# Hybrid SSD block on one Trainium2 core: the last three projection pairs ordered product by product, two projection tiles moved from the direct form into a pair, and three steps of the scan drawn forward

## Chip, core and metric

The kernel runs on one core of one Trainium2 chip. The metric is the device time of one execution in microseconds. Before the change it is 1902.68 us (median of 3 runs, 1902.15 to 1902.8).

## The reference, cut to what matters

`x` has 1024 rows (time) and 1024 channels, all in float32:

```
u = rmsnorm(x) @ w_in                       # 1024 x 10272 columns, split into:
z, xbc, dt, s_b, s_c, s_x, g_a, g_b         # 2048, 3072, 32, then five of 1024
xbc = silu(causal_conv4(xbc) + b);  xs, B, C = split(xbc)
y = chunked_scan(xs, softplus(dt), a, B, C) + d * xs
y = group_rmsnorm(y * silu(z)) ;            branch_a = y @ w_ssd_proj
branch_b = (s_b * causal_conv3(s_c * s_x)) @ w_sconv_proj
h = x + (sigmoid(g_a) * branch_a + sigmoid(g_b) * branch_b) @ w_o
out = final_norm(h + (silu(n @ w_gate) * (n @ w_up)) @ w_down),  n = rmsnorm(h)
```

## The kernel before

**Precision and tiling.** Every large product is made of float32r matmuls on operands split into a high and a low half (`split`, or `hi` and `lo` of a pair: ScalarE, ACT in the profile, copies the high half, VectorE, DVE, subtracts to get the low one). One 128x128 by 128x512 block costs three matmuls: high by high, high by low, low by high (`mmc`, lines 680 to 682, and `mm3`, lines 81 to 83). The order of instructions on each engine is the order in which the Python program issues them; nothing is reordered later.

**Pairs.** Two neighbouring tiles of 128 columns of `w_in` form a `Pair`, which is computed with a seven-product scheme of the Strassen-Winograd kind instead of eight: products 1, 2, 6, 5, 7, 3, 4 of four k-blocks each, so 12 matmuls in one *slot*. The stationary side of a product is a sum of weight blocks (A1, S1 to S4, A2), made in `sums` on DVE and split in `hi` and `lo`; the moving side is one of the operands `T` (B11, B21, B22, T1 to T4) made once from the normalized rows. Products 1, 6, 7 and 4 accumulate into one PSUM bank (`b`), 2 and 5, 3 into another (`d`); `ev` takes the partial result out after each product (on ACT after 1, 6, 5, 4, on DVE after 2, 7, 3), and the next product on that bank waits for it. `slots` is the list of (pair, product); `STAGES` says how many slots ahead the sums, high and low halves are issued. The first three pairs run product by product (all product 1, then all product 2, ...), all others pair by pair. After product 3 and product 4 a finished tile goes to `side`, whose steps `pump` issues, one per slot: for a `z` pair that is one SiLU on ACT and a store (`silu_z`).

**The operands T.** They are made while the first pairs run, by the generator `second_half`, of which the dictionary `turns` takes steps after given slots (slot 9: B22, slot 11: T3, slot 14: T4). A second generator of that name does the same for the FFN.

**Direct tiles.** The last two `z` tiles and the sixteen gate tiles (`g_a`, `g_b`) are computed in the plain way, 2 halves x 8 k-blocks x 3 matmuls each, after all pairs. Beside them run the scan's steps: 32 items (4 groups x 8 chunks), each with `part1` (transposes, decay matrix by eight Relu and one Exp on ACT, five to six DVE operations) and, a step later, `part2` (state product `poff`, new state `pst`, diagonal `pdg`). `part1(j)` also issues item j+1's Relu and Exp. Steps are spread evenly over the direct matmul groups of three:

```
due = turn[0] * SCAN_STEPS // (len(direct) * 2 * KT - 4)
```

with SCAN_STEPS = 65 and 18 direct tiles (284). The scan's first step (loads) is issued once before them. After the direct tiles come the two output projections, `w_o`, and the FFN.

**Pages.** All large SBUF tiles come from one pool of 47 pages; a tile's page comes free after its last reader.

Of the kernel before, what the change touches and what calls it, by code (L numbers as in the profile page):

```python
# [10 lines left out]
AF = mybir.ActivationFunctionType  # L11
ALU = mybir.AluOpType

P = 128
S = 1024
D = 1024
KT = D // P
# [22 lines left out]
def hybrid_block(ctx: ExitStack, tc: tile.TileContext, x, nmw, w_in, cw, cb, dtb, alog, dsk, snw,  # L40
                 wssd, scw, wsc, wo, nfw, wg, wu, wd, fnw, out):
    nc = tc.nc
    ET = mybir.EngineType
    ctx.enter_context(tc.manual_schedule(engines={ET.PE, ET.Activation, ET.DVE, ET.Pool, ET.SP}))
    x, w_in, out = x[0], w_in[0], out[0]
# [14 lines left out]
    def page(s, shape=(P, 1024), dt=F32):  # L60
        return pp.tile(list(shape), dt, tag="pg", name=nm(s))
# [112 lines left out]
    def wslab(w, c0, cols=P, r0=0):  # L174
        return Slab(w[r0:r0 + D, c0:c0 + cols].rearrange("(k p) f -> p k f", p=P), (P, KT, cols))
# [45 lines left out]
    def every(gen):  # L221
        for _ in gen:
            pass
# [387 lines left out]
    def silu_z(i):  # L611
        def f(u):
            nc.scalar.activation(u, u, AF.Silu)
            nc.scalar.dma_start(z_d[i], u)
            yield
        return f
# [207 lines left out]
    def put(name, pages):  # L824
        T[name] = []
        for pg in pages:
            T[name].append(split(pg, "t", HB))
            yield
# [78 lines left out]
                side.append(self.done[1](self.u2))  # L907
                self.u2 = self.b = None

    z_pairs = [Pair(i * P, (silu_z(i), silu_z(i + 1))) for i in range(0, 14, 2)]  # L910
    x_pairs = [Pair(XBC0 + i * P, (conv_silu(i), conv_silu(i + 1))) for g in range(G)
               for i in (4 * g, 4 * g + 2)]
    bc_pairs = [Pair(XBC0 + i * P, (conv_silu(i), conv_silu(i + 1))) for i in (16, 18, 20, 22)]
# [7 lines left out]
    while conv_p or free_p:  # L921
# [2 lines left out]
        if free_p:  # L924
            rest_p.append(free_p.pop(0))
    pairs = first + rest_p
    NF = len(first)
    slots = [(p, n) for n in (1, 2, 5, 6, 7, 3, 4) for p in first] + \
        [(p, n) for p in rest_p for n in ORDER]


    STAGES = {1: ((2, "A1", 3), (0, "A1", 2)), 2: (), 6: ((1, "S3", 3), (1, "S2", 3), (2, "S2", 3), (0, "S2", 2)),
# [1 line left out]
              4: ((2, "A2", 4), (0, "A2", 3))}  # L934
    when = {}
    for i, (p, n) in enumerate(slots):
        for stage, what, d in STAGES[n]:
            if p not in first or what not in ("S3", "A1"):
                when.setdefault(i - d, []).append((stage, i, p, what))
        if p in first and n == 5:  # L940
            when.setdefault(i - 4, []).append((1, i, p, "S3"))
# [4 lines left out]

    loaded = [0]

    def load_pairs(n):
        while loaded[0] < min(n, len(pairs)):  # L950
            pairs[loaded[0]].y.load()
            pairs[loaded[0]].x.load()
            loaded[0] += 1
# [4 lines left out]
        p.ev(n)  # L958


    z_held = []

    def z_raw(i):
        def f(ps, hf):
            if hf == 0:
                z_held.append((i, page("gt")))
            nc.scalar.activation(z_held[-1][1][:, hf * 512:hf * 512 + 512], ps, AF.Copy)
            if hf and len(z_held) == 2:
                for k, t in z_held:
                    nc.scalar.activation(t, t, AF.Silu)  # L970
                    nc.scalar.dma_start(z_d[k], t)
                z_held.clear()
        return f

    direct = [(wslab(w_in, i * P), z_raw(i)) for i in range(14, 16)]
    for j in range(KT):
        direct += [(wslab(w_in, GA0 + j * P), gate_raw(ga_d[j])), (wslab(w_in, GB0 + j * P), gate_raw(gb_d[j]))]
    scan_steps = scans()
# [2 lines left out]
    def pump_scan(n=1):  # L981
        for _ in range(n):
            next(scan_steps, None)
# [6 lines left out]
    def direct_lo(slab):  # L990
        V.tensor_sub(slab.hl[1], slab.st, slab.hl[0].bitcast(F32))
        slab.st = None

    def direct_tile(i):
        slab, ev = direct[i]
        wh, wl = slab.hl
        slab.hl = None
        for hf in range(2):
            ps = bank("pr")
            for k in range(KT):  # L1000
                bh, bl = half_b(f"B{k // 4 + 1}{hf + 1}", k % 4)
                mm3(ps, wh[:, k, :], wl[:, k, :], bh, bl, k == 0, k == KT - 1)
                turn[0] += 1
                due = turn[0] * SCAN_STEPS // (len(direct) * 2 * KT - 4)
                if due > turn[1]:
                    turn[1] = due
                    pump_scan()
                if k % 8 == 5:
                    pump_aux()
                if i + 1 < len(direct) and (hf, k) == (0, 1):  # L1010
                    direct_hi(direct[i + 1][0])
                if i + 1 < len(direct) and (hf, k) == (0, 7):
                    direct_lo(direct[i + 1][0])
                if i + 2 < len(direct) and (hf, k) == (0, 2):
                    direct[i + 2][0].load()
            ev(ps, hf)
# [147 lines left out]
    def ffn_phase():  # L1164
# [27 lines left out]
        def second_half(rows):  # L1192
            yield from fill(rows, raw1, 1, wcol)
            t1 = [page("t1", HB) for _ in range(2)]
            for k in range(2):
                V.tensor_add(t1[k], raw1[0][k], raw0[0][k])
            t2 = [page("t2", HB) for _ in range(2)]
            for k in range(2):
                V.scalar_tensor_tensor(t2[k], raw1[1][k], -1.0, t1[k], op0=ALU.mult, op1=ALU.subtract)
            raw0[0].clear()  # L1200
            for k in range(2):
                nc.gpsimd.dma_start(raw1[0][k], raw1[1][k], accum_op=ALU.add)
            every(put("T2", t2))
            yield
            every(put("T1", t1))
            yield
            every(put("T3", raw1[0]))
            yield
            V.tensor_sub(raw0[1][0], raw0[1][0], t2[0])
            every(put("B22", raw1[1]))  # L1210
            yield
            V.tensor_sub(raw0[1][1], raw0[1][1], t2[1])
            every(put("T4", raw0[1]))
            yield

# [324 lines left out]
    rows_sq_on("v", a0, "x")  # L1540
    a1 = rows_acc(xt[4:8], "x")
    del xt
    for p in first:
        p.x.load(nc.gpsimd)
    pc = bank("pc")
    nc.tensor.transpose(pc[:, 0:96], ra, ident[:96, :96])
    nc.tensor.transpose(pc[:, 96:176], rb, ident[:80, :80])
# [41 lines left out]
    rows_sq_on("a", a1, "x")  # L1589
    p0.ev(1)  # L1590
    p2.hi("A1")
    p2.lo("A1")
    p2.pe(1)
    for k in range(4, 8):
# [11 lines left out]
    def second_half():  # L1606
        t1, t2 = [[page("t1", HB) for _ in range(2)] for _ in range(2)]
        for k in range(KT):
            if k % 2 == 0:
                raw1[k // 4].append(page("br", HB))  # L1610
            turn_rows(r1, k)
            pt = turned.pop(k)
            o = k % 4 // 2, k % 2
            nc.scalar.activation(raw1[k // 4][o[0]][:, o[1], :], pt, AF.Copy, scale=nmc[:, k:k + 1])
            less = (raw0[0] if k < 4 else t1)[o[0]][:, o[1], :]
            V.scalar_tensor_tensor((t1, t2)[k // 4][o[0]][:, o[1], :], pt, nmc[:, k:k + 1], less,
                                   op0=ALU.mult, op1=ALU.subtract)
            if k == 3:
                raw0[0].clear()
                for j in range(2):  # L1620
                    nc.sync.dma_start(b12_d[j], raw1[0][j])
                every(put("T1", t1))
            if k == 7:
                every(put("T2", t2))
            yield
        yield
        every(put("B22", raw1[1]))
        yield
        for k in range(2):
            V.tensor_sub(raw1[0][k], raw1[1][k], raw1[0][k])  # L1630
        every(put("T3", raw1[0]))
        raw1[0].clear()
        raw1[1].clear()
        yield
        for k in range(2):
            V.tensor_sub(raw0[1][k], raw0[1][k], t2[k])
        every(put("T4", raw0[1]))
        raw0[1].clear()
        yield
# [3 lines left out]
    for i in range(7 * NF):  # L1643
        if i >= NF:
            slot(i)
        make(i)
        for _ in range(turns.get(i, 0)):
            next(gen, None)
        if i == 2 * NF - 1:
            steps_pe(0, 1)  # L1650
        if i == 4 * NF - 1:
            steps_pe(1, 0)
            steps_pe(1, 1)
        load_pairs((i + 11) // 7 + 1)
        if i >= 4 * NF + 2:
            pump()
    every(gen)
# [7 lines left out]
        V.tensor_copy(cols[:, 176:192], pd2[:, 0:16])  # L1665

    sums = all_weight_sums()
    n_slots = len(slots)
    for i in range(7 * NF, n_slots):
        slot(i)  # L1670
        if i == 7 * NF + 4:
            time_steps(steps_ps)
            del steps_ps[:]
        if i == 7 * NF + 13:
            d_skip_rows()
        if i == 7 * NF + 14:
            d_skip_columns()
        make(i)
        load_pairs((i + 11) // 7 + 1)
        pump()  # L1680
        if i % 3 == 0:
            next(sums, None)
        if i % 3 == 1:
            pump_aux()
        left = n_slots - 1 - i
        if left in (4, 3, 2):
            del T[{4: "T2", 3: "T1", 2: "T3"}[left]]
        if left == 9:
            b12 = [page("br", HB) for _ in range(2)]
            for k in range(2):  # L1690
                nc.sync.dma_start(b12[k], b12_d[k])
        if left == 7:
            direct[0][0].load()
        if left == 4:
            every(put("B12", b12))
        if left == 3:
            direct_hi(direct[0][0])
            direct[1][0].load()
        if left == 2:
            direct_lo(direct[0][0])  # L1700
            pump_scan()
    every(sums)
    del T["T4"], b12
# [40 lines left out]
```

## Time and profile before

| | us |
|---|---|
| median of 3 runs | 1902.68 |
| the profiled execution | 1902.65 |
| its span, first to last instruction | 1900.8 |
| PE busy | 1875.0 |
| DVE busy | 1304.4 |
| ACT busy | 966.7 |
| direct tiles, first to last matmul | 636.8 to 949.7 |

PE is TensorE, PEld its weight loads, POOL is GpSimd, SP is SyncE (which issues most loads). The granted TensorE clock is 0.999 of full speed. A line number is that of the kernel before; L865 and L869 are the helpers `hi` and `lo` of a pair, L76 and L77 those of `split`.

### The profile page before, as it was taken

Reading aid. Unit: us, or ns where it says so; the run is one execution under the profiler, and the core shown is the slowest. Engines: PE = TensorE matmul, PEld = TensorE weight load, DVE = VectorE, ACT = ScalarE, POOL = GpSimd, SP = SyncE. Lnnn points to the kernel's source line nnn. Section 1 sums busy time; section 2 is a strip of 40 time slices with the busy share of each in tenths; the row PEclk is TensorE's granted clock in tenths of the full one; section 3 lists DMA queues with packets and bytes.
Section 4 is the critical chain, followed back from the end, with each engine's and each line's share of the span. In section 5 each row is a group of like instructions: output and inputs, shape, how many; then the busy total and the mean of one; then the engine's idle time right before and its main releaser. Section 6 shows DMA issues by size and latency. Waiting matters only on the chain. (4 is left out here: it accounts for less than half of the span.)

```text
span 1900.8 us, 24126 instructions
## 1 busy us (share of the span) xinstructions
PE 1875.0 (99%) x8893; PEld 1541.8 (81%) x8893; DVE 1304.4 (69%) x1694; ACT 966.7 (51%) x1541; POOL 177.3 (9%) x204
## 2 busy tenths in 40 slices
PE   6999999999999999999999999999999999999998
PEld 5788888888888888888888888888888888888886
DVE  7667888778685588999978558876444444456465
ACT  5545454444443788878665454464333333335333
POOL 2010111010100000010010000102211221100000
PEclk9999999999999999999999999999999999999999
DMA  5197999978958676688899665928988888867562
GB/s 182 58 265 173 242 230 236 233 190 230 267 143 233 225 247 213 225 273 263 281 323 333 221 211 203 232 82 199 212 198 210 202 192 196 235 258 283 188 196 109
DMA packets 336150, 413.02 MB, mean 217 GB/s; under 512 B 16408, under 2 KB 217840, under 8 KB 336032
## 3 DMA queue, kind: packets, MB, share of 16 engines
q1 hardware_dynamic: 277296, 302.43, 49.0%
q0 software_dynamic: 49664, 76.27, 21.6%
q10 hardware_dynamic: 9072, 32.77, 4.3%
q8 instruction: 70, 1.15, 0.2%
q14 instruction: 48, 0.39, 0.1%
HBM read 320.56 MB, written 143.15 MB: 244 GB/s over the span
## 5 line engine op out<-in xcount | busy, mean ns | idle before, releaser
L77 DVE TENSOR_TENSOR wl<-ws,wh 128x1024 fp32r<-128x1024 f32 x77 | 94.0, 1221 | 121.6 <-ACT wh L76 121.6
L680 PE MATMUL gb<-qh,gh 128*128 128x512 f32 x432 | 168.7, 391 | 0.1
L681 PE MATMUL gb<-ql,gh 128*128 128x512 f32 x432 | 168.4, 390 | 0.0
L682 PE MATMUL gb<-qh,gl 128*128 128x512 f32 x432 | 168.3, 389 | 0.0
L682 PE MATMUL fb<-th,wl 128*128 128x512 f32 x352 | 137.2, 390 | 0.5 <-DVE wl L77 0.5
L680 PE MATMUL fb<-th,wh 128*128 128x512 f32 x352 | 137.2, 390 | 0.0
L681 PE MATMUL fb<-tl,wh 128*128 128x512 f32 x352 | 137.1, 389 | 0.0
L681 PE MATMUL gd<-ql,gh 128*128 128x512 f32 x324 | 126.3, 390 | 0.0
L680 PE MATMUL gd<-qh,gh 128*128 128x512 f32 x324 | 126.2, 389 | 0.0
L682 PE MATMUL gd<-qh,gl 128*128 128x512 f32 x324 | 126.2, 389 | 0.0
L76 ACT ACTIVATE qh<-cb 128x1024 fp32r<-128x1024 f32 x98 | 99.9, 1019 | 38.8 <-PE gb L681 17.2
L81 PE MATMUL pr<-th,wh 128*128 128x512 f32 x288 | 118.8, 413 | 0.0
L77 DVE TENSOR_TENSOR ql<-cb,qh 128x1024 fp32r<-128x1024 f32 x98 | 115.7, 1181 | 2.8 <-ACT qh L76 2.7
L83 PE MATMUL pr<-th,wl 128*128 128x512 f32 x288 | 112.8, 392 | 0.0
L82 PE MATMUL pr<-tl,wh 128*128 128x512 f32 x288 | 112.6, 391 | 0.0
L680 PE MATMUL fd<-th,wh 128*128 128x512 f32 x264 | 102.8, 389 | 0.0
L682 PE MATMUL fd<-th,wl 128*128 128x512 f32 x264 | 102.8, 389 | 0.0
L681 PE MATMUL fd<-tl,wh 128*128 128x512 f32 x264 | 102.8, 389 | 0.0
L74 DVE SCALAR_TENSOR_TENSOR gl<-ca,gh 128x1024 fp32r<-128x1024 f32 (+1 forms) x60 | 70.6, 1176 | 44.1 <-ACT gh L73 44.0
L681 PE MATMUL pb<-tl,wh 128*128 128x512 f32 x248 | 96.9, 391 | 1.9 <-DVE tl L77 1.9
L680 PE MATMUL pb<-th,wh 128*128 128x512 f32 x248 | 97.7, 394 | 0.5 <-ACT u L895 0.5
L865 ACT ACTIVATE wh<-ws 128x1024 fp32r<-128x1024 f32 x62 | 65.7, 1059 | 63.5 <-DVE ws L852 59.6
(330 smaller groups left out, 4744.4 us busy)
## 6 DMA issues: line engine op xcount, KB each, us to landing
ws<-in_w_in_dram SPq DMA_DIRECT2D x75, 512.0 KB, 5.8
ws<-in_w_gate_dram SPq DMA_DIRECT2D x77, 256.0 KB, 3.9
ws<-in_w_up_dram SPq DMA_DIRECT2D x77, 256.0 KB, 4.4
ca<-u_d SPq DMA_DIRECT2D x35, 512.0 KB, 5.2
ab<-ac_d SPq DMA_DIRECT2D x32, 512.0 KB, 5.7
xbc_g<-cv ACTq DMA_DIRECT2D x24, 512.0 KB, 6.7
ws<-ws POOLq DMA_DIRECT2D x22, 512.0 KB, 6.4
wd_d<-in_w_down_dram SPq DMA_DIRECT2D x20, 512.0 KB, 10.3
```

Of the source, the lines that this page charges most:

```text
L74: nc.vector.scalar_tensor_tensor(lo, src, -1.0, hi.bitcast(F32), op0=ALU.mult, op1=ALU.subtract)
L76: nc.scalar.activation(hi, src, AF.Copy)
L77: nc.vector.tensor_sub(lo, src, hi.bitcast(F32))
L81: nc.tensor.matmul(o, lh, rh, start=first, stop=False)
L82: nc.tensor.matmul(o, lh, rl, start=False, stop=False)
L83: nc.tensor.matmul(o, ll, rh, start=False, stop=last)
L680: nc.tensor.matmul(o, lh, rh, start=first, stop=False, skip_group_check=True)
L681: nc.tensor.matmul(o, lh, rl, start=False, stop=False, skip_group_check=True)
L682: nc.tensor.matmul(o, ll, rh, start=False, stop=last, skip_group_check=True)
L865: nc.scalar.activation(t[0], self.source(what), AF.Copy)
```

## The change

It has six parts.

1. The last `z` tiles, 14 and 15, become an eighth `z` pair; the direct list holds the gates alone (16 tiles), and `z_raw` goes.
2. The last three pairs (all `z`) run product by product: 1, 2, 6 of the three, then 5 and 3 of different pairs in turn, then 7, then 4. `STAGES` of 3 and 7 are swapped for them (3 now comes first and needs S4), `load_pairs` loads them a pair every two slots, and T2, T1, T3 are freed at other slots.
3. Four steps of the scan instead of one are issued in these slots, when 10, 6, 3 and 0 slots are left; 62 steps are spread over 252 groups beside the direct tiles.
4. In the mixer's `second_half` the two subtractions that make T3 (L1630) move from the step of slot 11 to the end of the step of slot 9, behind B22's split.
5. In the FFN's `second_half` both subtractions for T4 (L1209 and L1212) are issued ahead of B22's split.
6. The second weight tiles (`x`) of the first three pairs are loaded from ACT's queue, after the high half of the third pair, instead of from POOL's queue before the constants are transposed.

```diff
-    z_pairs = [Pair(i * P, (silu_z(i), silu_z(i + 1))) for i in range(0, 14, 2)]
+    z_pairs = [Pair(i * P, (silu_z(i), silu_z(i + 1))) for i in range(0, 16, 2)]
...
-    NF = len(first)
+    NF, NL = len(first), 3
     slots = [(p, n) for n in (1, 2, 5, 6, 7, 3, 4) for p in first] + \
-        [(p, n) for p in rest_p for n in ORDER]
+        [(p, n) for p in rest_p[:-NL] for n in ORDER] + \
+        [(p, n) for n in (1, 2, 6) for p in rest_p[-NL:]] + \
+        [(rest_p[k - NL], n) for k, n in ((0, 5), (1, 5), (0, 3), (2, 5), (1, 3), (2, 3))] + \
+        [(p, n) for n in (7, 4) for p in rest_p[-NL:]]
...
-        for stage, what, d in STAGES[n]:
+        for stage, what, d in STAGES[{7: 3, 3: 7}.get(n, n) if p in rest_p[-NL:] else n]:
...
-    def load_pairs(n):
+    def load_pairs(i):
+        n, late = (i + 11) // 7 + 1, i + 11 - 7 * (len(pairs) - NL)
+        if late > 0:
+            n = len(pairs) - NL + 1 + late // 2
...
-    direct = [(wslab(w_in, i * P), z_raw(i)) for i in range(14, 16)]
+    direct = []
...
-                due = turn[0] * SCAN_STEPS // (len(direct) * 2 * KT - 4)
+                due = turn[0] * (SCAN_STEPS - 3) // (len(direct) * 2 * KT - 4)
...
-            V.tensor_sub(raw0[1][0], raw0[1][0], t2[0])
+            for k in range(2):
+                V.tensor_sub(raw0[1][k], raw0[1][k], t2[k])
             every(put("B22", raw1[1]))
             yield
-            V.tensor_sub(raw0[1][1], raw0[1][1], t2[1])
...
-    for p in first:
-        p.x.load(nc.gpsimd)
...
     p2.hi("A1")
+    for p in first:
+        p.x.load(nc.scalar)
...
         every(put("B22", raw1[1]))
-        yield
         for k in range(2):
             V.tensor_sub(raw1[0][k], raw1[1][k], raw1[0][k])
+        yield
         every(put("T3", raw1[0]))
...
+    T_LAST = {12: "T2", 8: "T1", 3: "T3"}
+    EARLY = (10, 6, 3, 0)
...
-        if left in (4, 3, 2):
-            del T[{4: "T2", 3: "T1", 2: "T3"}[left]]
+        if left in T_LAST:
+            del T[T_LAST[left]]
...
         if left == 2:
             direct_lo(direct[0][0])
+        if left in EARLY:
             pump_scan()
```

## Rows read from the trace of the kernel before

**Rows 1.** The page, busy time of each engine, share of the span, instructions.

```profile
PE 1875.0 (99%) x8893; PEld 1541.8 (81%) x8893; DVE 1304.4 (69%) x1694; ACT 966.7 (51%) x1541; POOL 177.3 (9%) x204
```

**Rows 2.** PE's waits: who released it, us in total, times, longest.

```profile
PE pb L681 <- DVE tl L77: 1.9, 2, 1.1
...
PE poff L476 <- ACT st L483: 0.6, 1, 0.6
...
PE fb L682 <- DVE wl L77: 0.5, 1, 0.5
```

**Rows 3.** Timeline of PE where the direct tiles begin: start, duration.

```profile
636.84 0.39 PE L81 MATMUL pr<-th,wh 128*128 128x512 f32 x1
...
637.52 0.39 PE L81 MATMUL pr<-th,wh 128*128 128x512 f32 x1
```

**Rows 4.** Timeline of all engines, 12.4 to 13.6 us.

```profile
12.09 0.91 POOL L165 DMA_DIRECT2D ws<-in_w_in_dram  x1
...
12.30 0.95 DVE L137 TENSOR_SCALAR xn<-x,nr 128x512 f32<-128x512 f32 x1
...
13.17 0.95 DVE L137 TENSOR_SCALAR xn<-x,nr 128x512 f32<-128x512 f32 x1
```

**Rows 5.** Timeline of DVE, 15.9 and 34 to 36 us.

```profile
15.80 0.47 DVE L137 TENSOR_SCALAR xn<-x,nr 128x512 f32<-128x512 f32 x1
...
34.26 1.21 DVE L845 TENSOR_TENSOR ws<-ws,ws 128x1024 f32<-128x1024 f32 x1
```

**Rows 6.** Timeline of PE, its transposes of the first rows.

```profile
14.27 4.93 PE L1557 MATMUL pt<-ident,xn 128*128 128x128 f32 x30 [0.49 <-DVE xn L137]
```

**Rows 7.** Timeline of ACT, 8 to 10 us; ACTq is its issuing side.

```profile
8.36 1.30 ACTq L245 DMA_DIRECT2D x<-in_x_dram  x3
```

**Rows 8.** Timeline of DVE, 64 to 79 us (slots 9 to 12).

```profile
66.82 1.22 DVE L869 TENSOR_TENSOR wl<-ws,wh 128x1024 fp32r<-128x1024 f32 x1
...
69.83 1.23 DVE L869 TENSOR_TENSOR wl<-ws,wh 128x1024 fp32r<-128x1024 f32 x1 [1.19 <-ACT wh L865]
...
71.57 2.35 DVE L1630 TENSOR_TENSOR br<-br,br 128x1024 f32<-128x1024 f32 x2
```

**Rows 9.** Timelines of ACT and of PE, 72 to 76 us.

```profile
72.89 2.19 ACT L76 ACTIVATE th<-br 128x1024 fp32r<-128x1024 f32 x2
...
75.26 0.50 PE L681 MATMUL pb<-tl,wh 128*128 128x512 f32 x1 [0.76 <-DVE tl L77]
```

**Rows 10.** Timeline of DVE in the FFN's start.

```profile
1303.66 1.22 DVE L1212 TENSOR_TENSOR br<-br,t 128x1024 f32<-128x1024 f32 x1
```

**Rows 11.** Timeline of ACT, the scan's first steps.

```profile
640.10 2.43 ACT L399 ACTIVATE ab<-ab,pac 128x128 f32<-128x128 f32 x8
642.55 1.28 ACT L401 ACT_TABLE_LOAD   x1
643.85 1.06 ACT L401 ACTIVATE ab<-ab 128x1024 f32<-128x1024 f32 x1
...
649.38 1.06 ACT L401 ACTIVATE ab<-ab 128x1024 f32<-128x1024 f32 x1
...
656.36 0.58 ACT L483 ACTIVATE st<-pst 128x512 f32<-128x512 f32 x1
```

**Rows 12.** Timeline of DVE, the same steps.

```profile
645.10 0.29 DVE L444 TENSOR_TENSOR cbm<-pcb,caus 128x128 f32<-128x128 f32 x1 [2.93 <-ACT bh L437]
...
647.25 1.22 DVE L991 TENSOR_TENSOR wl<-ws,wh 128x1024 fp32r<-128x1024 f32 x1
```

**Rows 13.** Windows: busy time and instructions of PE, PEld, DVE, ACT, POOL.

```profile
800.00:950.00 150.00, 150.00 (x954) 123.60 (x953) 141.63 (x242) 116.08 (x275) 14.38 (x23) 1.00 0.82 275
```

**Rows 14.** Timelines of ACT and PE, the state of items 24 to 26.

```profile
885.51 0.58 ACT L483 ACTIVATE st<-pst 128x512 f32<-128x512 f32 x1
...
886.58 0.60 PE L476 MATMUL poff<-bc,st 128*128 128x128 f32 x4
...
896.45 0.72 PE L476 MATMUL poff<-bc,st 128*128 128x128 f32 x5
```

More of the change, by code (lines that the diff above doesn't have):

```diff
@@ L958, in slot @@
         p.ev(n)
[L961 to L973, printed above, removed]
-    direct = [(wslab(w_in, i * P), z_raw(i)) for i in range(14, 16)]
+    direct = []
     for j in range(KT):
@@ L1653, in hybrid_block @@
             steps_pe(1, 1)
-        load_pairs((i + 11) // 7 + 1)
+        load_pairs(i)
         if i >= 4 * NF + 2:
@@ L1678, in hybrid_block @@
         make(i)
-        load_pairs((i + 11) // 7 + 1)
+        load_pairs(i)
         pump()
```

## The prediction, made before the changed kernel was run

> **What bounds the kernel.** The page comes first: PE is busy for 1875.0 of 1900.8 us, DVE for 1304, ACT for 967 [rows 1]. So time goes only where PE gets less to do or waits less. PE's list of waits is the second view: all that it waits for after the first 20 us are single waits of a microsecond or less, and three of them touch this change: for the low half of T3 (one of the two under L681), for the scan's state, and for a weight's low half in the FFN [rows 2]. The third view is PE's timeline, and it corrects a trap: a matmul is drawn 0.39 us long, but the next but two starts 0.68 us later [rows 3], so one costs 0.227 us, and a slot of 12 costs 2.72. The remaining views are the timelines of DVE and ACT around the places that the change touches, since both work in program order and PE waits for whatever stands late in them. The sum is made against the profiled execution's 1902.65 us (its span of 1900.8 and 1.85 around it), 0.03 from the median.
>
> **Part 1, the eighth pair.** Two direct tiles are 2 x 2 x 8 x 3 = 96 matmuls, a pair is 7 x 12 = 84. Twelve fewer at 0.227 us: -2.7 us. By the drawn 0.39 us it would be -4.7; the starts decide. ACT also loses four copies and DVE one low half net, neither of which PE waits for.
>
> **Part 6, the early loads.** The rows show a half of the normalization (L137) that takes 0.95 us and ends just when a load issued by POOL does, twice in a row [rows 4]; the last one, after POOL's last issue, takes 0.47 [rows 5]. With the three `x` loads gone from POOL, the one at 12.30 still waits (for the third pair's `y`), the one at 13.17 no longer. PE's long run of transposes, released at 14.27 by that half [rows 6], starts some 0.57 us earlier (it needs the half's end, 13.64 rather than 14.12 or so, and what lay between); PE's wait for the first low half follows it. I take -0.6; the bounds are 0 and -1.5 (three halves at 0.48 saved). The Trainium skill says the same of the cause: in "SBUF — State Buffer", section "SBUF: two separate sides", VectorE in its two-port mode and GpSimd exclude each other for whole instructions. By that rule too a half is freed entirely or not at all, which these durations bear out. On ACT the three issues take 1.30 us on its issuing side, which runs beside the computing one [rows 7]; if it did not, ACT's next copy would come 1.3 us later, the upper bound for this part. The `x` tiles are first needed by the subtraction at 34.26 [rows 5], some 9 us after their new issue near 24; I price that at nothing. If DVE did have to wait there, PE's transposes behind it would be late next.
>
> **Part 4, T3's subtractions.** They go ahead of three things in DVE's queue: the low half at 66.82, the sum that lets ACT make the next pair's high half, and the low half at 69.83, for which DVE waited 1.19 us on ACT [rows 8]. In before the two subtractions (71.57, 2.28 from start to start) ran while ACT made the last of the high halves, and T3's own high half followed at 72.89 [rows 9]. Now the sum, the high half, the low half and the next sum all slide by 2.28, the high half of the third pair with them, and T3's split stands behind that on ACT. So T3's low half is ready 2.28 us later, not sooner, and the wait that ended at 75.26 (about 1.0 us) becomes 3.3: +2.2 us. The bounds are -1.0 (the wait goes altogether, if ACT or DVE has room that I do not see) and +2.3.
>
> **Part 5, the FFN's subtractions.** The second one, at 1303.66 [rows 10], goes in front of B22's split, where DVE idled for most of its length; T4's split and the weight's low half behind it come 0.9 us sooner, and the wait of 0.5 under L682 [rows 2] (0.6 with its restart) goes: -0.6, bounds 0 and -0.6.
>
> **Parts 2 and 3, the scan's steps among the last slots.** The order by product gives every bank at least as much time as before; the list of waits shows nothing there to win. The cost is the scan's: its second step occupies ACT from 640.10 to the end of the Exp at 649.38, 10.2 us, and the third step 5.5 us more [rows 11]; DVE sits at L444 until 5.0 us into the first [rows 12], and 2.15 us of work follow. Set the clock to zero where PE ends the last product 3 (6 slots left). DVE's add and the SiLU behind it take until 2.0, the ACT block until 12.2. PE has the three products 7 (8.2) and twice 0.76 of transposes, so product 4 of the first pair runs from 9.7 to 12.4. For the second pair ACT's high half of A2 stands behind the block (12.8) and DVE's low half follows (13.5): 0.6 of waiting. For the third, the take-out of product 7 stands on DVE behind the low halves of B12, whose high halves end on ACT at 15.2: it is done at 17.3, PE wants it at 15.8. With crumbs +2.2 us. Bounds: 0, if ACT runs ahead by a few slots more than I set, and +5, if the third step's 5.5 us get into the same path. Next, the state's copy (L483), for which PE waits already, 0.6 idle and 0.2 of restart [rows 2, 11]: now it stands behind the third step, three take-outs, three SiLUs and a table load, some 1.5 us behind PE, so +0.7; bounds -0.8 and +2.
>
> Of table loads the row shows 1.28 us, with the Exp at once behind [rows 11]; SiLU and Exp alternate twice in these slots. The Trainium skill, "ScalarE: Activation LUTs", sections "What ACT_TABLE_LOAD costs" and "Table sets: the hidden batching unit", speaks against such alternating and prices a switch at 2.66 us, of which 1.38 are a drain. By that page the sum would be 2.8 us higher; the row has no such drain, so the sum stays.
>
> **The denser scan.** 62 steps over 252 groups are one in 4.06 instead of 4.37; an item is two steps, so its period falls by 0.62 groups of 0.68, from 9.87 us (poff to poff [rows 14]) to some 9.45, 4.3% less. From 800 to 950 us DVE is busy for 141.6 of 150 [rows 13]; the same work gets about 143.6. It fits barely; the state's copy ends 0.49 us before PE takes it at 886.58 [rows 14], and in such places 0.4 less period and a growing lag show. I take +1.3 us. Bounds 0 and +5.9 (0.42 an item over 14 items, if none of DVE's gaps closes).
>
> **The sum.** -2.7 - 0.6 + 2.2 - 0.6 + 2.2 + 0.7 + 1.3 = +2.5, rounded up for steps left out: 1905.3 us.
>
> **Rivals.** *Everything is hidden*: DVE and ACT run ahead of PE by more than I set, so neither burst reaches it and the T3 wait and the state's wait vanish: -2.7 - 0.6 - 1.0 - 0.6 - 0.8 = -5.7, 1897.0 us. For it: all waits in before are short. Against it: the chain through ACT and DVE at 66 to 73 us is serial [rows 8, 9]. *DVE becomes the bound beside the direct tiles*: it decides from the point where its lag passes the 0.49 us at item 25, and the price is 5.9 instead of 1.3: 1909.9, slower. For it: 94% busy there already [rows 13]. Against it: gaps that partly close. *A table switch costs its drain too*: ACT's block and the copies behind it lengthen by 1.4 each time, 1908.1 us; no row speaks for it. The page named above is its source. *Page waits*: a new page whose last reader is late holds DVE or a load in the last slots, 1908 or so; no row shows one.
>
> **Chances and range.** The forecast 0.45, all hidden 0.20, DVE the bound 0.28, table drain 0.02, page waits 0.05. A measurement of this kernel can tell 0.2%, 3.8 us: faster is below 1898.9, slower above 1906.5. The forecast lies between, so faster 0.20, same 0.45, slower 0.35. The range takes in both outer cases to about their middle, 1897.0 to 1909.5; the forecast's own is 1902.5 to 1907.
>
> **What would show it.** 8881 matmuls for 8893. PE's long transposes start near 13.7. The low half of T3 releases PE near 77.0 instead of 75.26, after a wait near 3 us. No wait under L682 in the FFN. Waits of 0.5 to 1.5 us at product 4 of the second and third of the last pairs, released by DVE, and one near 1.5 at the first poff. Waits at poff of items 25 and 31, and DVE above 97% in the last third of the direct tiles. I am wrong if the T3 wait shrinks, if PE runs through the last slots without a wait, or if DVE makes PE wait at many poffs.

## The result, and the profile after

The changed kernel takes 1911.67 us (median of 6 runs, 1909.81 to 1916.19) against 1902.64 of before beside it: a ratio of 1.0048, 95% interval 1.0038 to 1.0058. It is slower, by 9.0 us, and 2.2 above the upper end of the range; the forecast was 1905.3. The profiled execution took 1916.19 us, 13.5 more than that of before, and is the slowest of the six, so its rows hold more than the median does.

First the page and PE's list of waits after (us in total, times, longest; not all lines), which answer to [rows 1, 2]:

```profile
PE 1879.6 (98%) x8881; PEld 1541.4 (81%) x8881; DVE 1309.8 (68%) x1704; ACT 969.4 (51%) x1544; POOL 174.7 (9%) x201
```

```profile
PE poff L476 <- ACT st L483: 3.6, 2, 2.7
...
PE pb L681 <- DVE tl L77: 1.9, 2, 1.1
PE pb L680 <- ACT th L76: 1.8, 1, 1.8
PE pb L680 <- DVE u L900: 1.7, 2, 1.3
```

PE executes 12 matmuls fewer and yet is busy 4.6 us longer: matmuls themselves got slower somewhere. PE's timeline shows where, behind the wait for T3:

```profile
75.25 0.49 PE L680 MATMUL pb<-th,wh 128*128 128x512 f32 x1 [1.81 <-ACT th L76]
76.51 0.50 PE L681 MATMUL pb<-tl,wh 128*128 128x512 f32 x1 [0.77 <-DVE tl L77]
...
77.78 0.63 PE L680 MATMUL pb<-th,wh 128*128 128x512 f32 x1
78.21 0.63 PE L681 MATMUL pb<-tl,wh 128*128 128x512 f32 x1
...
80.77 0.58 PE L681 MATMUL pb<-tl,wh 128*128 128x512 f32 x1
81.19 0.40 PE L682 MATMUL pb<-th,wl 128*128 128x512 f32 x1
```

From 77.78 to 81.19 eight matmuls start 0.427 us apart, where 15 would fit at 0.227: a loss of 8 x 0.2 = 1.6 us. The windows (busy time and instructions of PE, PEld, DVE, ACT, POOL, then the granted clock, DMA share, GB/s) give the clock, half of full speed, 1.2 GHz, in this stretch and in two more:

```profile
77.70:81.10 3.40, 3.40 (x10) 2.67 (x9) 0.52 (x1) 0.55 (x1) 0.00 (x0) 0.51 0.00 0
675.10:678.50 3.40, 2.97 (x11) 2.54 (x11) 1.88 (x4) 3.38 (x9) 0.00 (x0) 0.50 0.97 324
955.00:958.40 3.40, 3.40 (x20) 2.74 (x17) 3.26 (x7) 0.00 (x0) 0.00 (x0) 0.50 0.51 196
676.00:954.00 278.00, 273.53 (x1749) 224.29 (x1749) 254.22 (x435) 227.63 (x546) 18.21 (x28) 1.00 0.76 248
```

Each of the three is 3.41 us long. The first and the third begin within 1.3 us behind a wait of PE, the second in the last 0.45 us of one. The second and third cost 1.4 and 1.6 us against the same instructions at full clock in `after_again`, a second profiled execution of the change (below). By the Trainium skill, "TensorE: Matmul & The Clock Gate", section "HAM oscillation — how this bites in real kernels", the loss is half of the throttled time, by which one would estimate 1.7 us for each. The rows come close to it. Before had no such stretch until its last microseconds.

The waits at product 4 of the last three pairs, and the first matmul behind the third one:

```profile
653.37 0.47 PE L680 MATMUL pb<-th,wk 128*128 128x512 f32 x1 [0.48 <-DVE u L900]
...
660.87 0.47 PE L680 MATMUL pb<-th,wk 128*128 128x512 f32 x1 [1.26 <-DVE u L900]
...
663.77 0.39 PE L81 MATMUL pst<-xw,bh 128*128 128x512 f32 x1
```

They stand at the first and the third pair. From 653.37 the 36 matmuls take 10.40 us, where 8.2 would do at 0.227; with the 0.7 us of the first wait and its restart product 4 loses 2.9 us.

The waits at the scan, on PE's timeline (the poff of items 1, 25, 27 and 31, and the start of a tile):

```profile
675.53 0.79 PE L476 MATMUL poff<-bc,st 128*128 128x128 f32 x2 [2.72 <-ACT st L483]
...
897.54 1.16 PE L476 MATMUL poff<-bc,st 128*128 128x128 f32 x8 [0.91 <-ACT st L483]
916.97 1.16 PE L476 MATMUL poff<-bc,st 128*128 128x128 f32 x8 [1.00 <-ACT gt L657]
925.33 0.50 PE L81 MATMUL pr<-th,wh 128*128 128x512 f32 x1 [0.85 <-ACT gt L657]
...
953.71 1.16 PE L476 MATMUL poff<-bc,st 128*128 128x128 f32 x8 [1.70 <-DVE st L485]
```

What lay ahead of the first of them on ACT (start, duration; ACTq is its issuing side), which answers to [rows 11]:

```profile
667.35 0.58 ACT L906 ACTIVATE u<-pb 128x512 f32<-128x512 f32 x1
667.94 1.28 ACT L613 ACT_TABLE_LOAD   x1
669.24 1.06 ACT L613 ACTIVATE u<-u 128x1024 f32<-128x1024 f32 x1
...
673.42 1.06 ACT L613 ACTIVATE u<-u 128x1024 f32<-128x1024 f32 x1
...
674.88 0.60 ACT L483 ACTIVATE st<-pst 128x512 f32<-128x512 f32 x1 [0.40 <-ACT u L613]
```

Three take-outs, a table load and three SiLUs stand between the Exp and the 0.6 us copy that PE waits for. The waits at 917 and 925 come from one more place, ACT's wait of 5.2 us for a page that a store of POOL still held (in before ACT never waits for that store):

```profile
910.94 0.63 ACT L441 ACTIVATE xw<-xx 128x512 fp32r<-128x512 f32 x1 [5.23 <-DMA yt_d<-y]
```

And this is DVE in front of the last wait:

```profile
949.50 1.22 DVE L74 SCALAR_TENSOR_TENSOR gl<-ca,gh 128x1024 fp32r<-128x1024 f32 x1
950.64 1.22 DVE L77 TENSOR_TENSOR ql<-cb,qh 128x1024 fp32r<-128x1024 f32 x1
951.78 0.68 DVE L471 TENSOR_TENSOR st<-st,cd 128x512 f32<-128x512 f32 x1
952.38 0.68 DVE L477 TENSOR_TENSOR xx<-poff,eb 128x512 f32<-128x512 f32 x1
952.98 0.68 DVE L485 TENSOR_TENSOR st<-st,pst 128x512 f32<-128x512 f32 x1
```

L74 and L77 are the low halves of the first chunk *behind* the direct tiles; its first matmul, at 963.93, reads them 12 us later. They stand ahead of the state (L471, L485) that PE takes at 953.71.

### The profile page after: what moved, and what is told of

Same layout as the page of the kernel before. It is cut to its first block, busy times and chain, and to the rows that moved or that the text cites. A ratio compares the mean times of both kernels' runs of the same rounds, so it can differ in the third digit from the quotient of the medians.

```text
span 1914.3 us, 24111 instructions
## 1 busy us (share of the span) xinstructions
PE 1879.6 (98%) x8881; PEld 1541.4 (81%) x8881; DVE 1309.8 (68%) x1704; ACT 969.4 (51%) x1544; POOL 174.7 (9%) x201
## 5 line engine op out<-in xcount | busy, mean ns | idle before, releaser
L77 DVE TENSOR_TENSOR wl<-ws,wh 128x1024 fp32r<-128x1024 f32 x77 | 94.0, 1221 | 121.6 <-ACT wh L76 121.6
L77 DVE TENSOR_TENSOR ql<-cb,qh 128x1024 fp32r<-128x1024 f32 x98 | 115.6, 1179 | 1.7 <-ACT qh L76 1.6
L81 PE MATMUL pr<-th,wh 128*128 128x512 f32 x256 | 106.6, 416 | 0.9 <-ACT gt L657 0.9
L680 PE MATMUL pb<-th,wh 128*128 128x512 f32 x256 | 101.6, 397 | 2.3 <-ACT th L76 1.8
L680 PE MATMUL pb<-th,wk 128*128 128x512 f32 x256 | 100.0, 391 | 2.0 <-DVE u L900 1.7
L74 DVE SCALAR_TENSOR_TENSOR gl<-ca,gh 128x1024 fp32r<-128x1024 f32 (+1 forms) x60 | 70.5, 1174 | 44.2 <-ACT gh L73 44.1
L83 PE MATMUL pr<-th,wl 128*128 128x512 f32 x256 | 100.4, 392 | 0.0
```

Of the source, the lines that this page charges most:

```text
L74: nc.vector.scalar_tensor_tensor(lo, src, -1.0, hi.bitcast(F32), op0=ALU.mult, op1=ALU.subtract)
L77: nc.vector.tensor_sub(lo, src, hi.bitcast(F32))
L81: nc.tensor.matmul(o, lh, rh, start=first, stop=False)
L83: nc.tensor.matmul(o, ll, rh, start=False, stop=last)
L680: nc.tensor.matmul(o, lh, rh, start=first, stop=False, skip_group_check=True)
```

## The experiments

Ratios are to before, with 95% intervals; the median of before was 1902.8 to 1903.1 in each set.

**The parts alone.** `t3_alone` is before with part 4, `no_t3` the change without it:

```diff
         every(put("B22", raw1[1]))
-        yield
         for k in range(2):
             V.tensor_sub(raw1[0][k], raw1[1][k], raw1[0][k])
+        yield
         every(put("T3", raw1[0]))
```

> The kernel before with part 4 alone (T3's two subtractions moved into slot 9's step). First theory, serial queue: the wait for T3 grows from 1.1 to about 3.1 us, +2.0 us, and if the granted clock falls to its lower level behind that wait, as it does at 77.7 us in the changed kernel, another 1.6: 1904.6 to 1906.3 us, with the granted clock of the run telling which. Rival, the subtractions are out of the way sooner: the wait goes, 1901.6 us. Second rival, the wait was there from something else that the whole change did: 1902.6 us, unchanged.

> The changed kernel with part 4 alone undone. First theory, waits add up and a long one costs clock too: 2.0 us less, or 3.6 less where the clock fell: 1908.0 to 1909.7 us, no half-clock stretch near 78 us. Rival, all that matters is the dense scan beside the direct tiles: 1911.7 us, unchanged.

t3_alone took 1906.42 (1.0017, 1.0008 to 1.0026), no_t3 1909.65 (1.0034, 1.0022 to 1.0047). T3's waits in the first:

```profile
75.55 0.50 PE L680 MATMUL pb<-th,wh 128*128 128x512 f32 x1 [1.83 <-ACT th L76]
76.81 0.50 PE L681 MATMUL pb<-tl,wh 128*128 128x512 f32 x1 [0.76 <-DVE tl L77]
77.14 0.39 PE L682 MATMUL pb<-th,wl 128*128 128x512 f32 x1
77.37 0.39 PE L680 MATMUL pb<-th,wh 128*128 128x512 f32 x1
```

The waits are those of the change, and here no half clock follows: starts stay 0.23 apart. Of the 11 runs three (the profiled one among them) lie at 1904.4 to 1905.1 with a mean clock of 0.999, eight at 1906.1 to 1907.3 with 0.998: the means of the groups (1904.7 and 1906.7) are 2.0 us apart, near the price of one fall.

`no_early` issues one scan step early, as before, and 65 beside the 16 tiles; `parts56` is before with parts 5 and 6 alone:

```diff
-    EARLY = (10, 6, 3, 0)
+    EARLY = (2,)
...
-                due = turn[0] * (SCAN_STEPS - 3) // (len(direct) * 2 * KT - 4)
+                due = turn[0] * SCAN_STEPS // (len(direct) * 2 * KT - 4)
```

> The changed kernel with a single early scan step (two slots before the end, as before the change), so 65 steps over 252 groups. First theory, the scan's burst among the last slots costs 2.4 us there and 2.9 at the first poff (with the clock 1.6 more): these waits go, but the direct tiles lose more than the 5.1 us of now, some 7; together 1907 to 1909 us. Rival, DVE alone is the bound beside the direct tiles, and the early steps only relieve it: three steps of about 8 us of DVE work come back into the stage, and the time rises to 1914 us or more.

> The kernel before with parts 5 and 6 alone (FFN subtractions and the x loads on ACT's queue). First theory: 0.8 us less at the start and 0.6 less in the FFN, 1901.2 us. Rival, the gain at the start is lost again at the next waits of DVE and ACT: 1902.0 us; second rival, nothing: 1902.6 us.

parts56 took 1901.33 (0.9991, 0.9983 to 1.0000), as expected. no_early took 1918.99 (1.0083), 10 us above its theory and in the range of its rival, DVE as the bound. In it the waits at product 4 are gone and the first poff's is 0.3, so the early steps do cause them; at the poffs of items 25 and 31 PE waits far longer:

```profile
PE poff L476 <- DVE st L485: 5.3, 1, 5.3
PE poff L476 <- ACT st L483: 3.7, 2, 3.3
```

**First theory beside the tiles: DVE's rate.** `two_rates` spreads the 62 steps unevenly, `light_dve` leaves out the second of the two additions into y, `state_dve` moves one copy to DVE:

```diff
-                due = turn[0] * (SCAN_STEPS - 3) // (len(direct) * 2 * KT - 4)
+                t0 = turn[0]
+                due = t0 * 32 // 122 if t0 <= 122 else 32 + (t0 - 122) * 30 // 130
```

```diff
-        for i in range(2):
+        for i in range(1):
             o = slice(i * 2 * P, i * 2 * P + 2 * P)
```

```diff
-                nc.scalar.activation(ns, pst, AF.Copy)
+                (V.tensor_copy if j == 0 else lambda o, i: nc.scalar.activation(o, i, AF.Copy))(ns, pst)
```

> The changed kernel, with its 62 scan steps spread unevenly over the same 252 groups of the direct tiles: 32 in the first 122 (one in 3.8) and 30 in the last 130 (one in 4.3, about as before). The work of each engine is the same. Theory (the waits at the poffs of items 25 and 31 and at 917 and 925 us come from the period in the stretch behind item 16, where the norms come on top and DVE is above 97% busy): these four waits, 5.1 us with their restarts, shrink to under 1.5 in all, and the fall of the clock behind the last goes; 1906 to 1908.5 us against 1911.7. Rival (they come from the total of DVE's work beside the tiles, so a faster first half only moves the lag forward): waits of 3 us or more in all remain or appear before item 16, 1910 us or more.

> The changed kernel, leaving out half of the scan's last sums (L497: the second of the two additions into y, one 128x256 DVE instruction an item), so the output lacks those terms; DVE has some 0.37 us less in each period of 9.1 us, 4%. Nothing of the change itself is undone. Theory (DVE is the bound beside the direct tiles from item 16 on): the waits at the poffs of items 25 and 31 and around 917 to 925 us go (under 0.8 us in all), and the time falls by 3 to 7 us, to 1905 to 1908.5. Rival (those waits are late DMAs or ACT's lateness, and DVE's is only their consequence): at least 2 us of them stay, and the time is above 1909.5.

> The changed kernel, with the copy of the first item's state (L483, of the first item alone) on DVE in place of ACT, where it stood behind the Exp, three take-outs, three SiLUs and a table load. Theory (the wait of 2.7 us at the first poff is that queue on ACT, and DVE idles there): the wait goes whole (at most 0.8 stays), and the fall of the clock behind it with it; 1907 to 1909 us against 1911.7. Rival (ACT's block is late in any case, so that PE stops at the next thing that ACT owes it, the direct tiles' high half or the transposes' bank): a wait of 1.5 us or more remains at the first poff or within 10 us behind it, and the time stays above 1910.

two_rates took 1913.95 (1.0057): the four waits went, but 3.3 us of others came at 814 to 824, around item 17 (1.27 for a norm, 1.00 for a tile's low half, 1.03 for ACT's state copy). That is close to what its rival forecast, which puts the waits down to the total of DVE's work. light_dve takes work from DVE: 1912.55 (1.0051), no gain in time, and 1.3 us stayed at item 31. Its waits beside the tiles behind the first poff are 2.3 us in all, for 4.5 in the change; but no_t3, with DVE's work beside the tiles as in the change, has 2.5 too, so this isn't clearly the relief. The theory of the rate behind item 16 fell with both runs; against DVE's total light_dve speaks by its time alone. state_dve took 1908.74 (1.0033): the first poff's wait went whole, as its theory has it.

`best` and `best2` joined such edits with no_t3: `best` with the two rates and the early steps at 11, 8, 4 and 0 slots left, `best2` with the changed spots kept, 32 steps in 130 groups, 28 in 122, and two left for behind the tiles.

> The changed kernel with T3's subtractions as before (part 4 undone), the scan steps at two rates, the first state's copy on DVE, and the early steps with 11, 8, 4 and 0 slots left in place of 10, 6, 3 and 0. Theory: all that the change lost is in these four places, and each of them is one queue's lateness; what stays of the change is 12 matmuls (-2.7), the x loads (-0.8) and the FFN's subtraction (-0.6), with up to 1.5 of waits left over: 1898.5 to 1901 us, faster than before. Rival (the eighth pair cannot be had without waits beside the direct tiles, for the same scan work has 10% fewer groups to hide beside): 1903 us or more, with the waits moved to other items.

> The changed kernel with T3's subtractions as before, the first state's copy on DVE, 32 scan steps in the first 130 groups (one in 4.06, as the change has it), 28 in the last 122 (one in 4.36, as before) and the two steps left over beside the first two chunks behind the tiles. Theory (the change's loss is T3, the first poff, and the period behind item 16): waits of under 1 us in all beside the direct tiles, none at the first poff; 1901 to 1904 us. Rival (any placing of this scan work in 252 groups makes PE wait for DVE): 1.5 us or more of waits beside the direct tiles or just behind them, 1905 us or more.

Both missed their theories: 1910.24 and 1910.39. In best PE waits 3.85 us at a product of the last pairs, until ACT is in the decay block of a scan step; in best2 2.7 at a poff and 3.7 behind the tiles. Moving steps of the scan only moved the waits.

**The clock.** `clock_probe` and `clock_probe2` are before with holds of graded length in the FFN, where PE otherwise hardly waits (0.45 us once). The edit of the second, cut:

```diff
+                    if n in (2, 5) and u:
+                        hold_pe(m, cur["d"][1], 2 * u + (n == 5) - 2)
...
+                nc.tensor.transpose(o[:, 0:P], ident, ident)
+                V.tensor_copy(held_p[0], o[:, 0:P])
+                for _ in range(i // 2):
+                    V.tensor_copy(held_p[0], held_p[0])
...
+                nc.tensor.transpose(o[:, 0:P], held_p.pop(), ident)
```

> The kernel before, with 18 holds of PE of graded length put in the FFN, one in front of product 2 and one in front of product 5 of the units 1 to 9: a transpose into the fresh bank, a chain of 1 to 21 DVE copies on it, a transpose that reads the last copy; both are overwritten by the product. The output is unchanged. Theory (the fall of the clock is a price of a long wait of PE, whatever the work around it): holds that make PE wait more than about 1.9 us are mostly followed by some 3.4 us at half clock, holds of under 1.6 us never, as the six traces so far show (7 of 9 against 0 of 11). Rival (the fall belongs to the places, that is, to the start-up of the matrix work at 78, 675 and 955 us, and not to the wait): no hold in the FFN is followed by one. Under the theory the run is longer by the sum of the waits and about 1.6 us for each fall; under the rival by the waits alone.

> As clock_probe, with shorter holds: the first transpose stands in front of the product's first 12 matmuls, the one that reads the last DVE copy in front of its last 12, so some 2.7 us of the chain are covered; 20 holds with 0 to 9 extra copies, two of each, from some 0.8 us up to about 3. All 20 holds of the first probe (3.5 to 8.9 us) were followed by half clock. Theory (the fall's price comes with the length of PE's wait): holds under 1.6 us are never followed by a stretch of half clock, most over 1.9 us are, each of 3.4 us. Rival (any wait that stands in that place brings it): the short ones bring it too.

They took 2083.35 and 1973.31 us. In the first the holds (20; unit 10 had them too) came out at 3.5 to 8.9 us, and half clock follows all of them. Three of the second, on PE's timeline:

```profile
1439.24 0.33 PE L1227 MATMUL fd<-ident,cbm 128*128 128x128 f32 x1 [2.22 <-DVE cbm L1225]
...
1483.45 0.33 PE L1227 MATMUL fd<-ident,cbm 128*128 128x128 f32 x1 [2.49 <-DVE cbm L1225]
...
1620.02 0.33 PE L1227 MATMUL fd<-ident,cbm 128*128 128x128 f32 x1 [3.27 <-DVE cbm L1225]
```

```profile
1440.70:1444.10 3.40, 3.40 (x10) 2.62 (x9) 0.43 (x1) 0.69 (x1) 0.00 (x0) 0.50 0.26 101
...
1484.00:1487.40 3.40, 3.40 (x17) 2.77 (x16) 0.70 (x2) 1.58 (x2) 0.00 (x0) 1.00 0.45 172
1620.10:1623.50 3.40, 3.40 (x16) 2.83 (x17) 0.82 (x2) 1.58 (x2) 0.00 (x0) 1.00 0.36 139
```

The wait of 2.22 is followed by half clock, those of 2.49 and 3.27 are not. Of the 20 holds, none of the nine up to 1.96 us is, three of the six between 2.2 and 2.8, four of the five from 3.0 to 3.8. So the fall belongs to waits and not to places, and in these counts its chance grows with the wait; near 2.5 us it is even. The length of one wait is not all, though: T3's pair of waits, 1.8 and 0.5 to 0.8 us close together, is followed by half clock in eight of the ten traces that have it.

**What stayed open.** `after_again` is the change once more. `copies_last` puts the state's copy on DVE for all four groups and takes the last scan step out of the tiles; `b12_later` splits B12 at one slot left; `best3` joins both with no_t3:

```diff
-                nc.scalar.activation(ns, pst, AF.Copy)
+                V.tensor_copy(ns, pst)
...
-                due = turn[0] * (SCAN_STEPS - 3) // (len(direct) * 2 * KT - 4)
+                due = turn[0] * (SCAN_STEPS - 4) // (len(direct) * 2 * KT - 4)
...
```

> The changed kernel once more, for a second profiled execution of it. Theory (the page wait at 911 us, its two waits of PE behind it and some of the falls of the clock are of single executions; the waits at T3, product 4, the first poff and the poffs of items 25 and 31 are of the kernel): these five places show again within 0.5 us each, the waits at 917 and 925 do not, and one or two falls are there in place of three; median 1911 to 1912.5. Rival (the profiled execution was typical): the waits at 917 and 925 are there again.

> The changed kernel, with the copy of each group's first state (L483, four of 32 items) on DVE in place of ACT, and the last scan step taken out of the direct tiles to the first chunk behind them (61 steps over 252 groups). Theory (the wait at item 25 is ACT's queue in front of that copy, the one at 31 is the last step that follows half a period behind the one before; DVE's throughput has little to do with either): the waits at the first poff and at the poffs of items 25 and 31 all fall under 0.5 us, and the falls of the clock behind them with them; 1905.5 to 1907.5 us. Rival (DVE's throughput): one DVE copy more for each group makes DVE later, so waits of 1 us or more stay at poffs from item 17 on; 1908 us or more, as state_dve.

> The changed kernel, with the split of B12 with one slot left in place of four (its first reader is the second half of the first direct tile, some 8 us later). Theory (product 7's take-out on DVE stands behind the two low halves of B12, which wait for their high halves on ACT): the waits at product 4, 0.5 and 1.4 us, go down to under 0.5 in all; the time falls by 1 to 2 us, unless ACT's first state copy, which now stands behind B12's high halves too, is later by as much. Rival (the scan's Exp block alone makes these take-outs late): 1 us or more stays at product 4.

> The changed kernel with T3's subtractions as before, and the edits of copies_last and b12_later. Theory (four single places make up the loss, and their edits add): 1900 to 1903 us. Rival (the places are coupled by DVE's queue, so that what is freed in one is waited for in the next): 1905 us or more.

after_again: 1913.71, above its theory's range, with the waits at T3, product 4, items 1, 25 and 31 again and one fall for three. The page wait is there again too, as its rival has it, with PE's two waits behind it (the first two lines from PE's list, the third from ACT's timeline):

```profile
PE pr L81 <- ACT gt L657: 0.8, 1, 0.8
PE poff L476 <- ACT gt L657: 0.6, 1, 0.6
```

```profile
910.03 0.63 ACT L441 ACTIVATE xw<-xx 128x512 fp32r<-128x512 f32 x1 [4.92 <-DMA yt_d<-y]
```

So it belongs to the changed kernel and not to a single execution. b12_later: 1911.41, no gain; the wait for L900 fell to 0.5 in all, but the first tile now waits 0.76 for B12's low half and the first poff still 1.53. copies_last took 1916.77 (1.0071), best3 1915.88; both missed their theories. In copies_last the waits at the poffs of items 1 and 25 are gone, but this stands at item 31, on PE and on DVE:

```profile
955.11 2.05 PE L476 MATMUL poff<-bc,st 128*128 128x128 f32 x8 [6.42 <-DVE st L485]
```

```profile
946.89 1.22 DVE L74 SCALAR_TENSOR_TENSOR gl<-ca,gh 128x1024 fp32r<-128x1024 f32 x1 [3.29 <-ACT gh L73]
948.03 1.22 DVE L77 TENSOR_TENSOR ql<-cb,qh 128x1024 fp32r<-128x1024 f32 x1
949.16 0.68 DVE L442 TENSOR_TENSOR xx<-pxt,dtt 128x512 f32<-128x512 f32 x1
```

DVE idles for 3.3 us in front of L74, with the scan's item behind it in the queue: the first chunk's split, issued at the start of the last tile, now comes before the item's first half too. The Trainium skill has the rule in "Perfetto Trace Analysis", section "Tensor Engine Instruction (MATMUL, LD_WEIGHTS)": ACT, DVE and GpSimd take their queues strictly in order; this trace agrees, for L442 comes only after L74 and L77. From the rows, then, the cause of item 31's wait would be the split's place and not DVE's rate, which these edits test:

```diff
+                if i + 1 == len(direct) and (hf, k) == (0, 4):
+                    ms.ahead(3, 1)
...
-        ms.ahead(i - len(direct) + 4, i - len(direct) + 2)
+        ms.ahead(i - len(direct) + 4, 0)
```

`copies_split` is the change with this and the four copies on DVE, `best4` the same without part 4; `parts56_state` is parts56 with state_dve's edit.

> The changed kernel, with the copy of each group's first state on DVE and the split of the first chunk behind the direct tiles moved from the start of the last tile to its fifth group, that is, on DVE from in front of the last state's update to behind it. Scan steps and their number as in the change. Theory (the wait at item 31 is the two low halves L74 and L77, 2.3 us, in DVE's queue in front of the last state; those at the first poff and item 25 are ACT's late copy): all three waits fall under 0.5 us, and the falls of the clock behind them go: 1904 to 1907 us. Rival (DVE's throughput makes the last items late): 1 us or more stays at item 31 or appears at the first chunk behind the tiles; 1907.5 or more.

> copies_split with T3's subtractions as before. Theory (the causes add: T3 costs 2 to 4 us more): 1901 to 1904 us, 2 to 4 below copies_split, and no fall of the clock before the end. Rival (coupled places): within 1 us of copies_split.

> The kernel before with the x loads on ACT, the FFN's subtraction moved, and the first state's copy on DVE: no part of the change that touches the pairs or the scan. Theory (single waits add up where no queue is made longer): parts56's gain of 1.4 and the first poff's wait of 0.8 less: 1900 to 1901 us. Rival (DVE is as late there as ACT, or the freed wait comes back at the next bank): 1901.3 or more.

copies_split took 1903.82 us (1.0003, 0.9994 to 1.0012), 7.9 below the change, best4 1900.56 (0.9987, 0.9978 to 0.9996), parts56_state 1900.53 (0.9986, 0.9977 to 0.9995). The same stretch in best4, 676 to 954 us:

```profile
676.00:954.00 278.00, 278.00 (x1780) 229.56 (x1779) 262.55 (x454) 227.04 (x540) 19.64 (x30) 1.00 0.79 257
```

PE does not wait once, with DVE *busier* than in the change (262.55 us of 278 against 254.22): at 94% DVE carries the denser scan. The last 94 us of the direct tiles say it more sharply, in the change and in best4:

```profile
860.00:954.00 94.00, 89.53 (x573) 72.63 (x572) 88.45 (x148) 76.37 (x179) 8.37 (x13) 1.00 0.80 263
```

```profile
855.00:949.00 94.00, 94.00 (x603) 77.69 (x600) 91.97 (x159) 73.48 (x172) 8.54 (x13) 1.00 0.85 280
```

DVE is busy for 94% in the change, where PE waits, and for 98% in best4, where it does not. Of ACT's two page waits in the change (3.1 us at 834 and the one of 5.2 at 911) the second is gone in both runs; the first is still 3.1 us in best4, where it costs PE nothing, and 5.2 in copies_split, where PE waits 0.6 behind it. No run takes the page waits away alone. What best4 still waits for beyond before's waits is product 4, twice:

```profile
PE pb L680 <- DVE u L900: 1.7, 2, 1.2
```

## Why the prediction was wrong

| term | forecast | measured |
|---|---|---|
| 12 matmuls | -2.7 | x8881; -2.7 by the starts |
| x loads (part 6) | -0.6 | PE's first low half at 19.74, was 20.57: -0.8 in these two executions; over all kept traces nearer -0.4 |
| T3 (part 4) | +2.2 | waits 1.81 and 0.77, was 0.76: +2.0 with the restart; in time +3.4 alone, 3.3 from best4 to copies_split |
| FFN (part 5) | -0.6 | the wait is gone: -0.6 |
| scan among the last slots | +2.2 | 0.5 and 1.3 of waits, restarts and smaller ones: +2.9 by the starts |
| first poff | +0.7 | 2.72, was 0.6: +2.1 |
| denser scan | +1.3 | 0.9, 1.0, 0.85 and 1.7 of waits: +4.5, of them 1.85 behind the page wait (4.6 and 1.5 in after_again) |
| fall of the clock | not in the sum | 1.6, 1.4 and 1.6 in the profiled execution: +4.6 (one fall in after_again) |

The measured column makes 12.0; the restarts behind the waits of the denser scan bring most of what lacks to 13.5.

**What held.** The matmuls, the start, the FFN and T3's wait in its place; T3's comes in two parts, though, first for ACT's high half and then for DVE's low one. At product 4 the waits and the engine held, but they stand at the first and third of the last pairs and not at the second and third. "All hidden" fell with them, and the table drain too: at 667.94 the load takes 1.28 us and the SiLU starts at once.

**The step that failed first** is the term that was not there: each wait was priced by its length alone. A wait of some 2 to 3 us has a second price, 3.41 us at half clock or some 1.5 us lost, in some executions and not in others (behind probe holds of 2.7 to 3.8 us some stretches are twice as long). All of PE's waits in before, past its first 20 us, are near 1 us or less [rows 2], so its trace did not show one. The change makes three places of about this size: T3's and the first poff's, which were short waits before and which the forecast had itself put at 3.3 and 1.5 us, and item 31's, where PE did not wait before. In the profiled execution this term is the largest that was missed; in after_again, with one fall, the denser scan's is.

**First poff.** The mechanism was right (the copy behind take-outs, SiLUs and a table load), the size not: 2.1 for 0.7. That is just beyond the upper bound of +2. Taken away (state_dve), the time falls by 2.9.

**Denser scan.** Here the mechanism was wrong. The prediction read the 0.49 us at item 25 and DVE's 94% as a lag of DVE that grows [rows 13, 14]. best4 contradicts it: a busier DVE made nobody wait, and the sign that the forecast named, DVE above 97%, came there and not in the change. light_dve's time agrees. What it took for a rate are mostly two places in a queue: ACT's copy of a group's first state, and the next stage's low halves ahead of the last state on DVE. With both moved copies_split is 7.9 us faster, falls of the clock included. The rival "DVE the bound" gave 1909.9, nearer than the forecast, by the wrong cause. The rival "page waits" came in part, and not where it was put: ACT waits for a page beside the direct tiles, in both executions of the change, and PE's waits behind it are 1.85 and 1.5 us. Why they shrink when the two places are moved isn't shown. Whether DVE is the bound at 65 steps (no_early) was not tried with these two places mended, and stays open.

**Part 1 for itself.** best4, with the pair and the early steps, and parts56_state, without them, both stand at 1900.5: the 2.7 us of the matmuls are paid back at product 4, which loses 2.9 by the starts. Moving the early steps or B12's split did not get them.

## What to carry to other kernels

Before calling an engine the bound because it is busy and something near it is late, look at what stands directly in front of the late instruction in its queue: here a 0.6 us copy and two low halves that nobody needed yet cost more than a denser stage. Price a wait of TensorE of some 2 us or more with the half clock that may follow it, and expect such a kernel's times to spread. Of the nine kernels that rearranged the changed scan here, six were not faster than the change beyond what undoing part 4 gives; the three that were (state_dve, copies_split, and best4 with part 4 undone) left the steps where they were and moved only what stood late in a queue or in front of something late.

## What the hardware showed unexpectedly

A wait of TensorE as short as 1.70 us (953.71) was followed by 3.41 us at half clock, one of 3.27 (1620.02) was not. The spread of the runs goes with it: best4, without such waits, has 11 runs within 0.7 us (1900.4 to 1901.11), the changed kernel six within 6.4. It isn't all of the spread: of after_again's five runs one of 1910.16 has a mean clock of 0.998 and one of 1913.71 has 0.999.
